# A decoder layer on one core: the residual stream kept with features on partitions, the norms' sums on TensorE, and the last gate in block products

## The chip, the cores and the metric

One Trainium2 chip, one of its cores. The metric is the device time of one launch in microseconds (us), lower is better: the median of three runs. All inputs lie in HBM (DRAM) when the launch begins, and the output must be there at its end.

## The reference, cut to what matters

One layer (DEPTH 1, batch 1) works on x of 1024 tokens by 1024 features, all in float32:

```python
def rms_norm(x, g):
    return x * lax.rsqrt(jnp.mean(x * x, axis=-1, keepdims=True) + EPS) * g
def swiglu(h, w_gate, w_up, w_down):
    return (jax.nn.silu(h @ w_gate) * (h @ w_up)) @ w_down

x = x + 0.5 * swiglu(rms_norm(x, ffn1_norm), ffn1_w_gate, ffn1_w_up, ffn1_w_down)   # hidden width 2816
h = rms_norm(x, mix_norm)
...                                     # h @ w_in, two attentions of 8 heads of 64, two sigmoid gates
x = x + merged @ w_out
x = x + 0.5 * swiglu(rms_norm(x, ffn2_norm), ffn2_w_gate, ffn2_w_up, ffn2_w_down)
x = x + sigmoid(rms_norm(x, ple_norm) @ w_ple_gate) * (p @ w_ple_proj)              # p: 1024 x 256
```

So there are four norms over the features, each ahead of a matrix product, and the residual x is read and written by every stage.

## The kernel before, in words

**Numbers.** A float32 matrix is split into a rounded part (`hi`, written by ScalarE as fp32r) and the rest (`lo`, a subtraction, mostly on VectorE): `split` at L104, whose two instructions stand in the profile at L105 and L106. A product takes three passes, hi times hi, hi times lo and lo times hi, so one 128x512 result over four blocks of 128 features is 12 matmuls.

**Seven products.** The large products are cut into two by two blocks and done with seven block products instead of eight, from sums of blocks. `make_up` (L474) does this for products whose input is a normed x: for each block n of 256 output columns, products m = 1 to 7, of 12 matmuls each (L556), in the order of `up_order`. Block 0 alone is done with all eight (`plain`, L506, 24 matmuls per result). The moving operands of the seven products are sums of the four blocks of h (two halves of 512 tokens by two halves of the features): `combo_a` makes the blocks of the second half of tokens, `combo_t` and `combo_l` the operand of product 5, `combo_u` and `combo_s` those of products 6 and 7, `combo_d` and `combo_e` that of product 4. Of these, the sums and the lo parts run on VectorE (L581 for lo parts, L617, L618, L626, L631, L632, L645, L646), the hi parts on ScalarE. `prep` splits a stationary weight tile (L105, L106), and `sums` (L521 to L523) forms sums of weight blocks. `make_down` (L363) does the same for the products that end in the residual: matmuls at L454, with the result added to the residual X from PSUM by VectorE at L462 (`evict`).

**The layout.** X is held as two halves of 512 tokens, each a tile of 128 tokens by 4 by 1024 features, tokens on partitions. A norm sums over one partition's row: ScalarE squares with a running sum (`norm_stat`, L215), GpSimd adds EPS and takes the power -0.5 on one column (L219, L220), VectorE multiplies by the gain (`norm_mul`, L223, 128x1024). The products need features on partitions, so `turn` (L228) transposes each normed tile on TensorE into PSUM, eight 128x128 transposes per 128 tokens, and the split into hi and lo reads PSUM (L105, L248 on ScalarE, L106, L253 on VectorE).

**The stages.** There are four entries, places where a norm feeds a `make_up` or, at the last, a plain product: FFN1 at the start (`first_entry`, L1426), the mix stage at about 650 us (`mix_start`, L1188), FFN2 at about 1520 us (`second_entry`, L1531), and the last stage at about 2160 us (`ple_start`, L1606). In the last three, the norm of the first half runs beside the last three products of the down product before it (`up_step`, L311: i counts the seven products, t the four results in one), and the second half's norm beside the first products after it (`up_first`, L330; `products`, L268). In `first_entry`, x comes in by pieces of 512 KB on SyncE's queue. The gain row is spread over the partitions by two fp32 matmuls (L190), and four bf16 matmuls (L204) follow. The last stage has no block products: `ple_steps` (L1586) does 16 results of 24 matmuls each at L1598, the last of them cut in pieces of 256, 128 and 128 columns, and finishes each with a sigmoid, a multiplication by a projection of p (from DRAM, L1582), an addition of X and an output DMA of 256 KB or less (L1601 to L1604).

**What sets the order.** The program order of each engine is the order of the code: every stage named here runs under a manual schedule. TensorE takes its matmuls strictly in that order, and so do VectorE, ScalarE and GpSimd; a wait of one instruction holds all behind it on its engine. The input and output DMAs go out from SyncE in order.

Of the kernel before, what the change touches and what calls it, by code (L numbers as in the profile page):

```python
# [18 lines left out]
P = 128  # L19
S = 1024  # L20
# [16 lines left out]
def tile_hybrid_decoder_layer(  # L37
# [118 lines left out]
    nc.vector.memset(mhalf[:], -0.5)  # L156

    xd = dp.tile([S, D], F32, name="x_mid")
    pd = dp.tile([S, D], F32, name="p_proj")
# [4 lines left out]

    def norm_begin(X, gain, first=None):
        if first is None:
            gB = slot("PT", [P, D])
            nc.sync.dma_start(gB[:], gain.partition_broadcast(P))
        else:
            gB = first["g"]  # L170
        return {"x": X, "g": gB, "hi": slot("H", [P, KD, 512], F32R), "lo": slot("H", [P, KD, 512], F32R), "h": {}, "r": {}}

    def combo_begin(X, gain, first=None, row=False):

        if first is None:
            gB = slot("PT", [P, D])
            if row:
                nc.scalar.dma_start(gB[0:1, :], gain.unsqueeze(0))
            else:
                nc.sync.dma_start(gB[:], gain.partition_broadcast(P))  # L180
            return {"x": X, "g": gB, "h": {}, "r": {}, "B": [slot("H", [P, 2, 4, 512], F32R) for _ in range(2)]}
        return {"x": X, "g": first["g"], "h": {}, "r": {}}

    def spread(gB):

        ones = slot("T", [1, P])
        nc.vector.memset(ones[:], 1.0)
        banks = [bank("sc") for _ in range(2)]
        for i, ps in enumerate(banks):
            pe(nc.tensor.matmul(ps[:], ones[:], gB[0:1, i * 512:i * 512 + 512], start=True, stop=True))  # L190
        for i, ps in enumerate(banks):
            nc.vector.tensor_copy(gB[:, i * 512:i * 512 + 512], ps[:])
# [3 lines left out]
    def busy(n):  # L196

        if not zero:
            zero.append(slot("T", [P, 512], BF16))
            nc.vector.memset(zero[0][:], 0.0)  # L200
            return
        ps = bank("av")
        for _ in range(n):
            pe(nc.tensor.matmul(ps[:], zero[0][:, 0:P], zero[0][:], start=True, stop=True))  # L204

    def norm_pre(N, t, tag="PT"):
        norm_stat(N, t, tag)
        norm_mul(N, t)

    def norm_stat(N, t, tag, first=False):  # L210
        xt = N["x"][:, t, :]
        h = N["h"][t] = slot(tag, [P, D])
        ss = stat([P, 1], "ss")
        rs = N["r"][t] = stat([P, 1], "rs", 8)
        nc.scalar.activation(h[:], xt, AF.Square, scale=D ** -0.5, accum_out=ss[:])  # L215
        if first:
            nc.scalar.activation(ss[:], ss[:], AF.Copy, bias=EPS)
        else:
            nc.gpsimd.tensor_scalar(ss[:], ss[:], EPS, None, ALU.add)  # L219
        nc.gpsimd.tensor_tensor(rs[:], ss[:], mhalf[:, 0:1], ALU.pow)  # L220

    def norm_mul(N, t):
        nc.vector.scalar_tensor_tensor(N["h"][t][:], N["x"][:, t, :], N["r"].pop(t)[:], N["g"][:], ALU.mult, ALU.mult)  # L223

    def turn(h, b, ps):
        for c in range(4):
            k = 4 * b + c
            pe(nc.tensor.transpose(ps[:, c * P:(c + 1) * P], h[:, k * P:(k + 1) * P], identf[:]))  # L228
        return ps[:].rearrange("p (c t) -> p c t", c=4)

    def norm_post(N, t, new_bank):
        h = N["h"][t]
        cs = slice(t * P, (t + 1) * P)
        for b in range(2):
            v = turn(h, b, new_bank())
            if "B" in N:
                split(N["B"][b][:, 0, :, cs], N["B"][b][:, 1, :, cs], v, nc.scalar, nc.vector)
            else:
                ks = slice(4 * b, 4 * b + 4)
                split(N["hi"][:, ks, cs], N["lo"][:, ks, cs], v, nc.scalar, nc.vector)  # L240

    def norm_high(N, t, new_bank):

        cs = slice(t * P, (t + 1) * P)
        N["v"] = N.get("v", {})
        N["v"][t] = [turn(N["h"][t], b, new_bank()) for b in range(2)]
        for b in range(2):
            nc.scalar.copy(N["B"][b][:, 0, :, cs], N["v"][t][b])  # L248

    def norm_low(N, t):  # L250
        cs = slice(t * P, (t + 1) * P)
        for b, v in enumerate(N["v"].pop(t)):
            nc.vector.tensor_sub(N["B"][b][:, 1, :, cs], v, f(N["B"][b][:, 0, :, cs]))  # L253

    def posts(N, at, new_bank):
        side = {}
        for t, i in enumerate(at):
            side.setdefault(i, []).append(lambda t=t: norm_post(N, t, new_bank))
        return side

    def halves(N):
        return [lambda a, k, n=n: n[("hi", "lo")[a]][:, k, :] for n in N]

    def finished(X, dst, half, t):
        row = half * 512 + t * P
        nc.sync.dma_start(dst[row:row + P, :], X[half][:, t, :])

    def products(F, rest=()):  # L268

        F.load(2)  # L270
        for i in range(2):
            F.plain(1, 0, (i,))
            for q in rest[i:i + 1]:
                F.a(q)
            F.prep(1, 1 + i)
        F.prep(1, 5)
        ps = F.product(1, 1)
        F.t(0)
        F.evict(1, 1, ps)
        F.t(1)  # L280
        F.l(0)
        ps = F.product(1, 2)
        F.t(2)
        F.prep(2, 1)
        F.l(1)
        F.t(3)
        F.l(2)
# [12 lines left out]
        F.s(3, 6)  # L300
        F.prep(1, 6)

    def up_begin(N, X, gain, F, i):

        if i == 3:
            N.append(combo_begin(X[0], gain))
            N.append(combo_begin(X[1], None, N[0]))
        elif i == 6:
            F.load(0)

    def up_step(N, X, dst, F, i, t):  # L311

        if i == 4:
            finished(X, dst, 0, t)
            norm_stat(N[0], t, ("WL", "WL", "WL", "WH")[t])
        elif i == 5:
            norm_mul(N[0], t)
        elif i == 6:
            finished(X, dst, 1, t)
            if t == 3:  # L320
                norm_post(N[0], 2, ps1)
            norm_stat(N[1], t, ("PT", "PT", "WH", "KL")[t])
            if t:
                if t < 3:
                    norm_mul(N[1], t - 1)
                norm_post(N[0], (None, 0, 1, 3)[t], ps1)
            if t == 2:
                F.prep(0, 1)

    def up_first(N, F):  # L330

        norm_mul(N[1], 2)
        F.load(1)
        F.a(0)
        norm_mul(N[1], 3)
# [1345 lines left out]
```

## Time and profile before

| what | number |
|---|---|
| median of three runs | 2263.56 us (2262.96 to 2263.61) |
| the profiled execution's own time | 2264.1 us |
| its span, first to last instruction | 2262.4 us |
| TensorE (PE) busy | 2235.7 us, 99% |
| VectorE (DVE) busy | 1486.8 us, 66% |
| ScalarE (ACT) busy | 989.3 us, 44% |
| GpSimd (POOL) busy | 801.2 us, 35% |
| mean granted TensorE clock | 0.999 of full speed |

The profile holds one execution, with the start and the duration of every instruction. A row of its timeline reads: start in us, duration or, where several instructions in a row are drawn together, their common length, engine, line, operation, tiles written and read, shape, count (x12), and in brackets the idle time of the engine ahead of it with what ended it. Two matmul records overlap, since a matmul's end is modelled; the pace of matmuls is read from the distance of starts. PEld is TensorE's weight load, which runs beside the matmuls. A busy share says how long an engine worked, not that it held up the end; for this the rows with brackets are read.

### The profile page before, as it was taken

To read this page: it belongs to the slowest core of one execution; us is meant where nothing else is said; L and a number is where in the kernel's file an instruction comes from. 1 tells how busy PE (TensorE), PEld (TensorE's weight loads), DVE (VectorE), ACT (ScalarE), POOL (GpSimd) and SP (SyncE) were. 2 spreads that over 40 slices of the span, in tenths; PEclk is the share of its full clock that TensorE was granted. 3 is DMA by queue.
4 is the path that set the end of the run, shared out by engine and by line. 5 is a ranking of instruction groups with operands and counts; after the bars stand their busy time and mean duration, and the time that the engine had idled before them with its cause. 6 is when DMAs were issued, how large, how long until landed. Compare 5 with 4: busy or idle time off the path is not lost. (4 is left out here: it accounts for less than half of the span.)

```text
span 2262.4 us, 30810 instructions
## 1 busy us (share of the span) xinstructions
PE 2235.7 (99%) x11402; PEld 1900.8 (84%) x11402; DVE 1486.8 (66%) x2303; ACT 989.3 (44%) x1788; POOL 801.2 (35%) x803
## 2 busy tenths in 40 slices
PE   8999999999999999999999999999999999999999
PEld 6888888888888899999898888888888888888888
DVE  8845555688888325666678875889655555778753
ACT  6333333333364445555566663345333333433431
POOL 2444444300011336565567664410544444200121
PEclk9999999999999999999999999999999999999999
DMA  4232323484233333233323366821423232756132
GB/s 140 102 117 85 125 84 125 145 311 172 84 131 113 127 109 110 85 113 85 85 66 91 106 196 232 283 106 55 140 89 121 84 126 84 268 191 217 59 102 85
DMA packets 188936, 291.23 MB, mean 129 GB/s; under 512 B 28393, under 2 KB 104553, under 8 KB 188786
## 3 DMA queue, kind: packets, MB, share of 16 engines
q1 hardware_dynamic: 188784, 289.26, 38.5%
q8 instruction: 90, 1.47, 0.3%
q14 instruction: 60, 0.49, 0.1%
q10 hardware_dynamic: 2, 0.00, 0.0%
HBM read 193.50 MB, written 78.94 MB: 120 GB/s over the span
## 5 line engine op out<-in xcount | busy, mean ns | idle before, releaser
L454 PE MATMUL ps<-H,H 128*128 128x512 f32 x2184 | 497.7, 389 | 1.2 <-DVE X L462 1.2
L454 PEld LDWEIGHTS ps<-H,H 128*128 128x128 f32 x2184 | 409.4, 188 | 86.6 <-issue 2.0
L556 PE MATMUL ps<-H,WL 128*128 128x512 f32 x1116 | 264.9, 389 | 0.8 <-ACT WL L105 0.8
L556 PEld LDWEIGHTS ps<-H,WL 128*128 128x128 f32 x1116 | 209.4, 188 | 44.6 <-ACT WL L105 1.2
L556 PE MATMUL ps<-H,Q 128*128 128x512 f32 x612 | 146.0, 389 | 0.0
L462 DVE SCALAR_TENSOR_TENSOR X<-ps,X 128x512 f32<-128x512 f32 x168 | 109.1, 687 | 50.9 <-PE ps L454 50.9
L556 PEld LDWEIGHTS ps<-H,Q 128*128 128x128 f32 x612 | 114.9, 188 | 23.8
L556 PE MATMUL ps<-X,WL 128*128 128x512 f32 x552 | 132.6, 389 | 0.0
L139 POOL TENSOR_TENSOR WL<-RAW,WH 128x512 fp32r<-128x512 f32 (+1 forms) x84 | 98.5, 1194 | 69.1 <-ACT WH L129 43.2
L556 PEld LDWEIGHTS ps<-X,WL 128*128 128x128 f32 x552 | 103.6, 188 | 21.5
L1121 DVE TENSOR_TENSOR PT<-ps,PT 128x512 fp32r<-128x512 f32 (+1 forms) x160 | 100.0, 627 | 30.9 <-ACT PT L1115 29.7
L799 PE MATMUL ps<-WH,H 128*128 128x256 f32 x768 | 116.1, 288 | 0.8 <-ACT RN L864 0.8
L807 PE MATMUL ps<-H,WH 128*128 128x512 f32 x384 | 115.1, 406 | 0.0
L219 POOL TENSOR_SCALAR ss<-ss 128x1 f32<-128x1 f32 x28 | 9.0, 323 | 296.1 <-ACT WL L215 231.9
L1139 PE MATMUL ps<-PT,X 128*128 128x256 f32 (+1 forms) x640 | 102.7, 286 | 6.9 <-DVE PT L1121 5.8
L556 PE MATMUL ps<-H,PT 128*128 128x512 f32 x456 | 108.9, 389 | 0.0
L1115 ACT CAST PT<-ps 128x512 fp32r<-128x512 f32 (+1 forms) x160 | 87.1, 548 | 42.2 <-PE ps L1113 40.7
L1139 PEld LDWEIGHTS ps<-PT,X 128*128 128x128 f32 x640 | 90.3, 190 | 17.6 <-DVE PT L1121 10.8
L799 PEld LDWEIGHTS ps<-WH,H 128*128 128x128 f32 x768 | 101.4, 190 | 2.7 <-ACT RN L864 1.2
L556 PEld LDWEIGHTS ps<-H,PT 128*128 128x128 f32 x456 | 85.5, 188 | 17.8
L355 POOL TENSOR_TENSOR PT<-GF,RN 128x512 f32<-128x512 f32 x20 | 33.6, 1682 | 184.9 <-DVE GF L710 184.9
L1067 POOL TENSOR_TENSOR T<-T,l 128x128 f32<-128x128 f32 (+3 forms) x64 | 73.2, 1148 | 72.1 <-DVE l L1066 70.0
(436 smaller groups left out, 4889.0 us busy)
## 6 DMA issues: line engine op xcount, KB each, us to landing
hidden<-PT SPq DMA_DIRECT2D x40, 512.0 KB, 3.0
WH<-in_ffn_w_gate_dram SPq DMA_DIRECT2D x38, 512.0 KB, 5.5
Q<-hidden SPq DMA_DIRECT2D x24, 512.0 KB, 5.5
hidden<-RN SPq DMA_DIRECT2D x22, 512.0 KB, 2.6
KH<-in_ffn_w_up_dram SPq DMA_DIRECT2D x20, 512.0 KB, 6.2
KL<-in_ffn_w_up_dram SPq DMA_DIRECT2D x20, 512.0 KB, 6.8
T<-in_ffn_w_down_dram SPq DMA_DIRECT2D x20, 512.0 KB, 7.5
X<-in_x_dram SPq DMA_DIRECT2D x16, 512.0 KB, 10.2
```

The costliest lines, as they stand in the source:

```text
L139: ins = eng_lo.tensor_sub(lo[part], raw[part], f(hi[part]))
L219: nc.gpsimd.tensor_scalar(ss[:], ss[:], EPS, None, ALU.add)
L355: eng.tensor_add(s12[:, 0, :], g1[:, 1, :], g2[:, 1, :])
L454: pe(nc.tensor.matmul(groups[g][t][:], act[:, a, k, t * P:(t + 1) * P], wt[:, b, k, :], start=(fresh and n == 0), stop=(i in (6, 1, 4) and ...
L462: nc.vector.scalar_tensor_tensor(xs, groups[g][t][:], scale, xs, ALU.mult, ALU.add)
L556: pe(nc.tensor.matmul(ps[:], hl[:, a, k, :], rhs(m, b, k), start=(first and i == 0), stop=(final and i == 11), skip_group_check=True))
L799: pe(nc.tensor.matmul(ps[:, :n], hT[t // 4](a, k)[:, (t % 4) * P:(t % 4 + 1) * P], w[k // 4][b][:, k % 4, :n], start=(i == 0), stop=(i == ...
L807: pe(nc.tensor.matmul(ps[:], w[a][:, k, :], hT[half](b, k), start=(i == 0), stop=(i == 23)))
L1067: nc.gpsimd.tensor_mul(T[:, :n], T[:, :n], l[:].broadcast_to([P, n]))
L1115: high = nc.scalar.copy(pt[:, 0, :width], ps[:, :width])
L1121: ins = nc.vector.tensor_sub(pt[:, 1, :width], ps[:, :width], f(pt[:, 0, :width]))
L1139: pe(nc.tensor.matmul(o, lh, r, start=(kpair == c and i == 0), stop=(kpair == 0 and i == 3)))
```

## The change

The residual is held with features on partitions from the first load to the output: X is now `[P, KD, 512]` for each half, KD = 8 blocks of 128 features by 512 tokens. The host transposes x, p and the output and reorders the gains; in DRAM the middle residuals, the projection of p and the output have the features outermost.

```diff
 def product / matmuls (make_down; the operands change places)
-pe(nc.tensor.matmul(groups[g][t][:], act[:, a, k, t * P:(t + 1) * P], wt[:, b, k, :], ...
+pe(nc.tensor.matmul(groups[g][t][:], wt[:, b, k, t * P:(t + 1) * P], act[:, a, k, :], ...
 def evict
-xs = X[half][:, t, d * 512:d * 512 + 512]
+xs = X[half][:, d * 4 + t, :]
```

The norm's sum now runs over partitions. ScalarE squares each 128x512 block; GpSimd (VectorE for the last) adds the eight squares; four fp32 matmuls by a column of ones give the sums of 512 tokens as a 128x4 tile; VectorE adds EPS, GpSimd takes the power; and four TensorE transposes of the broadcast column give a 128x512 tile in PSUM whose rows are all alike. VectorE multiplies X by gain and this row, block by block. No normed data are transposed.

```diff
-    def turn(h, b, ps):
-        for c in range(4):
-            k = 4 * b + c
-            pe(nc.tensor.transpose(ps[:, c * P:(c + 1) * P], h[:, k * P:(k + 1) * P], identf[:]))
...
+    def norm_sq(N, k, eng=nc.gpsimd):
+        d = norm_at(N, k)
+        nc.scalar.activation(d, N["x"][:, k, :], AF.Square, scale=D ** -0.5)
...
+            eng.tensor_add(N["acc"], N["acc"], d)
...
+    def norm_sum(N, ps):
+        acc = N.pop("acc")
+        for t in range(4):
+            pe(nc.tensor.matmul(ps[:, t:t + 1], acc[:, t * P:(t + 1) * P], ones1[:], start=True, stop=True))
+        rs = N["r"] = stat([P, 4], "rs")
+        nc.vector.tensor_scalar(rs[:], ps[:, 0:4], EPS, None, ALU.add)
+        nc.gpsimd.tensor_tensor(rs[:], rs[:], mhalf[:, 0:4], ALU.pow)
...
+    def norm_row(N, ps):
+        rs = N.pop("r")
+        for t in range(4):
+            pe(nc.tensor.transpose(ps[:, t * P:(t + 1) * P], rs[:, t:t + 1].broadcast_to([P, P]), identf[:]))
+        N["row"] = ps
...
+    def norm_mul(N, k):
+        nc.vector.scalar_tensor_tensor(norm_at(N, k), N["x"][:, k, :], N["g"][:, k:k + 1], N["row"][:], ALU.mult, ALU.mult)
```

The combos of `make_up` now go by feature block k instead of token block q, on 128x512 blocks in SBUF. `combo_b` (the lo parts) is split off `combo_a`, one of its two subtractions going to GpSimd; `combo_u` is split in u (in `products` on GpSimd) and v; and v, the hi and the lo part of product 6's operand follow each other for each k.

```diff
 def products
-        F.plain(0, 1)
-        F.u(0)
-        F.u(1)
-        F.s(0, 6)
-        F.s(1, 6)
-        F.prep(2, 2)
-        F.plain(1, 1)
-        F.u(2)
-        F.u(3)
-        F.s(2, 6)
-        F.s(3, 6)
+        for k in range(4):
+            F.t(k)
+            if k:
+                F.l(k - 1)
+                F.u(k - 1, nc.gpsimd)
+        F.l(3)
+        F.u(3, nc.gpsimd)
+        F.plain(0, 1)
+        for k in range(4):
+            F.v(k)
+            F.s(k, 6)
+        F.prep(2, 2)
+        F.plain(1, 1)
         F.prep(1, 6)
```

`first_entry` loads x in pieces of 256 KB, one per feature block, squares each, and issues one fp32 matmul of 128x512 with a zero stationary operand on each piece that has come (`busy`, L232 of the kernel after); both bf16 and gain matmuls of before are gone. The last stage becomes a `make_up` of four column blocks: block 0 with `plain`, 96 matmuls, and three blocks of 84. Its results are finished by `finish`, a multiplication and an addition with tiles of the projection and of the residual (which now makes a round trip through DRAM) that a DMA brings in: for blocks 0 to 2 on GpSimd over 128x1024, for the last block on VectorE over 128x512.

```diff
+        def finish(n, i, e, hs=slice(0, 2), eng=nc.gpsimd, more=True):
+            pt, xt = T[n, i]
+            eng.tensor_mul(e[:, hs], e[:, hs], pt[:, hs])
+            eng.tensor_add(e[:, hs], e[:, hs], xt[:, hs])
+            nc.sync.dma_start(out[0, (2 * n + i) * P:(2 * n + i + 1) * P, :].rearrange("p (h n) -> p h n", h=2)[:, hs], e[:, hs])
...
+            seqn = up_order(4)
+            for s, (n, m) in enumerate(seqn):
+                evict(n, m, F.product(n, m))
```

TensorE at the start of the program, before. PT, WL and Y hold normed tokens, H the operands, L506 is `plain`:

```order
L190 MATMUL ps_110<-PT_101,T_107 128x512
L204 MATMUL ps_158<-T_105 128x512
L228 MATMUL ps_163<-identf,PT_130 128x128 x4
...
L228 MATMUL ps_211<-identf,PT_151 128x128 x4
L506 MATMUL ps_237<-H_103,WL_189 128x512 x12
L506 MATMUL ps_237<-H_104,WL_228 128x512 x12
L228 MATMUL ps_289<-identf,Y_220 128x128 x4
...
L506 MATMUL ps_338<-H_103,WL_258 128x512 x12
```

The same place after the change. X is the residual, PT and Q the sums of squares of the two halves, rs the 128x4 column, L482 is now `plain`:

```order
L232 MATMUL ps_117<-X_101,T_115 128x512 x8
L199 MATMUL ps_161<-ones_86,PT_134 128x1 x4
L208 MATMUL ps_169<-identf,rs_166 128x128 x4
L482 MATMUL ps_209<-H_175,WL_184 128x512 x12
L482 MATMUL ps_209<-H_176,WL_199 128x512 x12
L482 MATMUL ps_259<-H_175,WL_206 128x512 x12
L199 MATMUL ps_272<-ones_86,Q_225 128x1 x4
L482 MATMUL ps_259<-H_176,WH_222 128x512 x12
L208 MATMUL ps_296<-identf,rs_277 128x128 x4
L532 MATMUL ps_335<-H_175,PT_280 128x512 x12
```

The first product moved behind the sum and the row of the whole first half, where before it stood behind transposes of single token blocks; and the second half's sum and row stand between whole products.

VectorE in `products` of FFN1, before, from the second `combo_u` on. Q, KH and KL hold the second half's blocks, RN and GF the sums, H_493 is product 6's operand:

```order
L631 TENSOR_TENSOR Q_308<-Q_308 128x512
L632 TENSOR_TENSOR Q_308<-Q_308,RN_425 128x512
L581 TENSOR_TENSOR H_493<-Q_288,H_493 128x4x128
L581 TENSOR_TENSOR H_493<-Q_308,H_493 128x4x128
L106 TENSOR_TENSOR WL_498<-WH_335,WL_498 128x512
L631 TENSOR_TENSOR KH_351<-KH_351 128x512
```

The same place after (L601 is v, L554 a lo part, H_427 product 6's operand):

```order
L601 TENSOR_TENSOR Q_225<-Q_225,RN_378 128x512
L554 TENSOR_TENSOR H_427<-Q_225,H_427 128x512
L601 TENSOR_TENSOR Q_227<-Q_227,RN_378 128x512
L554 TENSOR_TENSOR H_427<-Q_227,H_427 128x512
L601 TENSOR_TENSOR KH_230<-KH_230,GF_387 128x512
L554 TENSOR_TENSOR H_427<-KH_230,H_427 128x512
```

The four u of before left VectorE, and each lo part now follows the v that it reads, with a hi part on ScalarE between them.

GpSimd from the first power on, after the change (L202 the power, L221 lo parts of the first half, L191 the sum of squares of the second, L554 lo parts of product 3's operand, L598 u):

```order
L202 TENSOR_TENSOR rs_166<-rs_166,mhalf 128x4
L221 TENSOR_TENSOR H_176<-PT_154,H_176 128x512
L191 TENSOR_TENSOR Q_225<-Q_225,Q_227 128x512
...
L202 TENSOR_TENSOR rs_277<-rs_277,mhalf 128x4
L554 TENSOR_TENSOR T_303<-Q_225,T_301 128x512
...
L554 TENSOR_TENSOR T_304<-KL_233,T_302 128x512
L598 TENSOR_TENSOR Q_225<-Q_225 128x512
...
L598 TENSOR_TENSOR KL_233<-KL_233 128x512
```

Before, GpSimd did only one-column work in this place (L219, L220), and its next 128x512 operation was a weight sum at L526. Now 15 operations of 128x512 stand there: 2 of L221, 5 of L191, 4 of L554 and 4 of L598.

More of the change, by code (lines that the diff above doesn't have):

```diff
@@ L184, in spread, with norm_begin @@
[L184 to L192, printed above, removed]
+    def norm_begin(X, i, tags):
+        return {"x": X, "g": gains[:, i, :], "tags": tags, "s": {}}
@@ L200, in busy @@
             nc.vector.memset(zero[0][:], 0.0)
+            zero.append(bank("av"))
             return
[L202 to L220, printed above, removed]
@@ L261, in halves @@
[L261 to L275, printed above, removed]
-        F.prep(1, 5)
[L277 to L283, printed above, removed]
+        pe(nc.tensor.matmul(zero[1][:], zero[0][:], src, start=True, stop=True))
@@ L330, in up_first @@
+            for k in ((0, 1), (2, 3, 4), (5, 6), (7,))[t]:
+                norm_low(N[0], k, nc.gpsimd if k in (4, 5) else nc.vector)
     def up_first(N, F):
[L332 removed]
         F.load(1)
+        F.prep(0, 2)
+        F.plain(0, 0, (0,))
+        norm_sum(N[1], bank("sc"))
+        F.prep(0, 5)
+        F.prep(0, 4, nc.gpsimd)
+        F.plain(0, 0, (1,))
+        norm_row(N[1], bank("av"))
         F.a(0)
[L335 to L337 removed]
+        F.plain(1, 0, (0,))
@@ L1457, in first_entry @@
+        norm_sum(N[0], bank("pt"))
+        norm_row(N[0], bank("pf"))
+        for k in range(4):
+            norm_mul(N[0], k)
+            norm_high(N[0], k)
+        F.prep(0, 1)
+        for k in range(4):
+            norm_low(N[0], k)
+        for k in range(4, 8):
+            norm_mul(N[0], k)
+            norm_high(N[0], k)
         F.prep(0, 2)
-        norm_stat(N[1], 1, "Y")
+        for k in range(4, 8):
+            norm_low(N[0], k, nc.gpsimd if k in (5, 7) else nc.vector)
+        F.prep(0, 5)
```

500 lines of the change are left out of this document (237 added, 263 removed).

## The prediction, made before the changed kernel was run

> **What bounds the kernel now.** I read the page's busy line first, then the list of what each engine waited for, then TensorE's timeline.
>
> ```profile
> PE 2235.7 (99%) x11402; PEld 1900.8 (84%) x11402; DVE 1486.8 (66%) x2303; ACT 989.3 (44%) x1788; POOL 801.2 (35%) x803
> ```
>
> ```profile
> PE ps L1139 <- DVE PT L1121: 5.8, 13, 1.3
> PE ps L1113 <- DVE PT L1121: 4.3, 6, 1.2
> PE ps L190 <- DMA PT<-in_ffn_norm_dram: 3.6, 1, 3.6
> PE ps L228 <- DVE H L106: 2.0, 3, 1.0
> PE ps L506 <- DVE H L253: 1.3, 1, 1.3
> ```
>
> Out of 2262.4 us TensorE idles 27, and the longest waits (total, times, longest) lie in the attention, which the change leaves alone. So the kernel is bound by TensorE, and a saving counts only if operands still come in time. VectorE's 66% is an average. At the FFN1 entry, where the change moves most, it is full (columns: PE, PEld, DVE, ACT, POOL):
>
> ```profile
> 20.00:40.00 20.00, 20.00 (x106) 16.89 (x105) 19.14 (x32) 14.23 (x32) 4.60 (x3) 1.00 0.26 80
> 40.00:60.00 20.00, 19.23 (x86) 15.58 (x85) 18.61 (x30) 10.69 (x20) 0.00 (x0) 1.00 0.00 1
> ```
>
> There VectorE works 19 of 20 us just to keep up, and GpSimd nothing. That is the place to watch.
>
> **TensorE's own work.**
>
> ```profile
> 22.17 1.91 PE L228 MATMUL ps<-identf,Y 128*128 128x128 f32 x16
> 23.83 2.99 PE L506 MATMUL ps<-H,WL 128*128 128x512 f32 x12
> 53.93 5.74 PE L556 MATMUL ps<-H,WL 128*128 128x512 f32 x24 [0.77 <-ACT WL L105]
> 59.50 2.88 PE L556 MATMUL ps<-X,WL 128*128 128x512 f32 x12
> 2165.25 1.20 PE L1598 MATMUL ps<-WH,H 128*128 128x512 f32 x4
> 2250.63 0.40 PE L1598 MATMUL ps<-WH,H 128*128 128x256 f32 x2
> 2258.59 0.39 PE L1598 MATMUL ps<-PT,H 128*128 128x128 f32 x2
> ```
>
> Sixteen transposes take 23.83 − 22.17 = 1.66 us, 0.104 each; 24 matmuls of 128x512 about 5.44, 0.2267 each (12 in 2.72). In the entries of mix, FFN2 and the last stage 192 transposes go: −20.0. The last stage's 360 matmuls of 128x512 and the three narrower pieces (2250.63 to 2258.8: 8.2) are 81.6 + 8.2 = 89.8; 96 + 3 x 84 = 348 are 78.9: −10.9. Added are six half-norms of 4 fp32 matmuls by one column and 4 transposes. A 128x1 matmul is in no row; I price its two records like transposes (12 x 0.104 = 1.25; from 0.4, only the transposes counted, to 3.1 if a record costs as much as a 512 one): +1.3 each, +7.8. Sum of work: −23.1. Were a row's duration taken for its cost, these transposes would be worth more: the Trainium skill, "TensorE: Matmul & The Clock Gate", Part 4, puts one PE transpose in a kernel at about 275 ns. This trace agrees with that as a record's length (16 end 1.91 us after the first began) but not as pace; by 275 ns the 192 would be 52.8 us and my total 33 lower, as an estimate. I go by the pace.
>
> **The price on VectorE and GpSimd.** The seven products' operands are made by VectorE, by dependent 128x512 operations:
>
> ```profile
> 35.09 0.69 DVE L617 TENSOR_TENSOR RN<-Q,H 128x512 f32<-128x512 f32 x1
> 35.81 0.69 DVE L618 TENSOR_TENSOR RN<-RN,H 128x512 f32<-128x512 f32 x1
> 36.42 0.69 DVE L617 TENSOR_TENSOR RN<-Q,H 128x512 f32<-128x512 f32 x1
> 109.14 0.62 ACT L105 CAST WL<-WH 128x512 fp32r<-128x512 f32 x1
> ```
>
> An operation starts 0.72 after the one that it reads, else 0.61. A cast on ScalarE is 0.62. From `norm_row` of the second half to the product (1,6), VectorE now has in program order: 8 `norm_mul` (4.9), 4 lo parts (2.4), 5 splits of weights (3.1; 6 in the last three entries, 3.7), 3 sums (2.2), one eviction (0.6), 8 subtractions of `combo_t` (5.3), 4 lo parts of product 5 (2.4). Then comes the new loop of v, hi on ScalarE, lo, each waiting for the one before: 0.69 + 0.04 + 0.62 + 0.04 + 0.61 = 2.0, four times, 8.0. v of the next block stands behind lo of this one, so ScalarE's cast can't be covered. Together 28.9.
>
> New on GpSimd in this stretch are 8 operations of 128x512, 4 lo parts (L554) and 4 u (L598). They are not free to VectorE:
>
> ```profile
> 107.81 0.69 DVE L106 TENSOR_TENSOR WL<-KH,WL 128x512 fp32r<-128x512 f32 x1
> 109.72 1.29 POOL L356 TENSOR_TENSOR PT<-PT,GF 128x512 f32<-128x512 f32 x1
> 109.80 1.76 DVE L106 TENSOR_TENSOR WL<-WH,WL 128x512 fp32r<-128x512 f32 x1 [1.31 <-ACT WL L105]
> 110.97 1.75 POOL L357 TENSOR_TENSOR PT<-GF 128x512 f32<-128x512 f32 x1
> 111.49 1.78 DVE L106 TENSOR_TENSOR WL<-KL,WL 128x512 fp32r<-128x512 f32 x1
> 114.72 0.69 DVE L690 TENSOR_TENSOR RN<-RN,ps 128x512 f32<-128x512 f32 x1 [1.46 <-ACT RN L689]
> ```
>
> The same L106 takes 0.69 alone and 1.76 beside a GpSimd operation; one that reads PSUM (L690) is not held. So each GpSimd operation costs VectorE 1.07, 0 to 8.6 for eight; two of the eight lie beside `norm_mul`, which reads PSUM, so 6.5. With 1.2 for two last casts: 28.9 + 6.5 + 1.2 = 36.6, and 37.2 in the last three entries. There TensorE has 120 matmuls in the same stretch (72 of `plain`, products (1,1), (1,2), (1,5), (2,1)), 27.2. It will idle 10.0.
>
> **Mix, FFN2, last stage.** Two smaller waits come in each. `norm_sum` puts an instruction into VectorE's queue (L201) behind the splits of the next down operand, 128x1024 each:
>
> ```profile
> 445.10 4.17 DVE L106 TENSOR_TENSOR H<-RAW,H 128x1024 fp32r<-128x1024 f32 x2
> 446.04 2.15 POOL L356 TENSOR_TENSOR KH<-KH,GF 128x512 f32<-128x512 f32 x1
> 449.19 2.30 DVE L106 TENSOR_TENSOR H<-KH,H 128x1024 fp32r<-128x1024 f32 x1
> 660.82 1.28 DVE L581 TENSOR_TENSOR H<-Q,H 128x512 fp32r<-128x512 f32 x2
> 5.89 0.56 POOL L220 TENSOR_TENSOR rs<-ss,mhalf 128x1 f32<-128x1 f32 x1 [4.03 <-ACT ss L217]
> ```
>
> Four splits at about 1.2 undisturbed (two operations of 512 are 1.28), an eviction 0.7, L201 and the power 0.8: 6.1 beside 12 matmuls, 2.7, and some start-up: 2.6 idle, 0 to 4, with `norm_row`, a down result of 12 matmuls and its eviction queued behind on TensorE. The second half's sum costs 0.7 likewise. So 2.6 + 0.7 + 10.0 = 13.3 idle for each entry. What idled there before, 2.0 (L228 row), goes. Mix: −6.7 (64 transposes) + 2.6 + 13.3 − 1.0 = +8.2. FFN2: the same, +8.2. Last stage: −6.7 − 10.9 + 2.6 + 13.3 = −1.7. Besides, blocks 0 to 2 are finished there by 12 GpSimd operations of 128x1024. The rows at 445 to 449 show VectorE's 1024 at 2.1 to 2.3 instead of 1.2 beside such work, so 12 x 1.0 = 12 at the most, 0 at the least; VectorE has some 30 operations (20 us) in 41 us of matmuls, so a third of the holds hits idle time: +8. And the end gets longer:
>
> ```profile
> 2255.03 5.27 SPq L1604 DMA_DIRECT2D out_dram<-KH  x3
> ```
>
> Before, 3.6 us lay between the last matmul and the end, with pieces of 64 KB and operations of 0.29. Now the last results are 128x512 (sigmoid 0.62, two operations 0.7, 256 KB), while block 2's two 1024 operations hold them (1.0 each) and their 512 KB goes ahead on SyncE: +5, from 1 to 8. Last stage and end: +11.3.
>
> At nothing I cost the swap of operands at L454 (as many matmuls of the same shape), the squares in pieces on ScalarE, and the residual's way through DRAM in the last stage, under this cover:
>
> ```profile
> 2165.00:2250.00 85.00, 84.91 (x392) 70.48 (x391) 31.61 (x42) 19.71 (x31) 13.74 (x12) 1.00 0.35 118
> ```
>
> ```profile
> Q<-hidden SPq DMA_DIRECT2D x24, 512.0 KB, 5.5
> ```
>
> ScalarE works 20 of 85 us there and the DMA engines 35%; a tile asked for one result ahead (5.4 us of matmuls) about covers the 5.5 us of a 512 KB load, and if not, it is GpSimd's `finish` that is late, not TensorE.
>
> **The first entry.**
>
> ```profile
> 3.58 3.75 PE L190 MATMUL ps<-PT,T 1*128 1x512 f32 x4 [3.58 <-DMA PT<-in_ffn_norm_dram]
> 9.30 1.06 ACT L215 ACTIVATE PT<-X 128x1024 f32<-128x1024 f32 x1
> 9.49 1.66 PE L228 MATMUL ps<-identf,PT 128*128 128x128 f32 x8 [0.35 <-DVE PT L223]
> 10.99 1.04 PE L228 MATMUL ps<-identf,WL 128*128 128x128 f32 x8
> 15.01 2.11 PE L506 MATMUL ps<-H,WL 128*128 128x512 f32 x8 [0.24 <-ACT H L248]
> ```
>
> The first half of x is in by 9.3. Eight fp32 matmuls are 16 records; four take 3.7 us at the start, 0.9 each, and the pace doubles at about 10.7 (the transposes at 9.49 against those at 10.99). From 4.4, 7 records by 10.7, 9 more at 0.45: 14.7 (12.5 if the clock is up sooner). Sum 0.9, L201 and power 0.8, row 0.5: 16.9. Four `norm_mul` with casts and a weight cast, 3.6: first product at 20.5, before 15.01. Its second part needs 13 VectorE operations (7.9) and casts from 16.9 on, and one more wait: 27.3. ScalarE's squares of the second half stand behind weight casts that wait for VectorE's last lo parts: first pair at 31.6. Then five GpSimd additions (1.37), two on VectorE (1.5): 39.9. Before that, TensorE has run out at about 33. Sum 1.0, 12 matmuls 2.7, row 0.5: 44.1. Plus the chain of 36.6: product (1,6) at 80.7. Before it began at 53.93 behind the same products: **+26.8**.
>
> **Sum.** 26.8 + 8.2 + 8.2 + 11.3 = +54.5 on the profiled 2264.1: 2318.6. The median is 0.5 below that execution: **2318**, 2.4% slower.
>
> **Rivals.**
> 1. *TensorE cools in the new gaps.* Its pace doubles only 7.1 us after the first matmul (3.58 to 10.7), and in this trace no gap after the start was longer than 1.3, so nothing shows what a gap of 3 to 7 us does. If it halves the pace for the next stretch: the sum, 12 matmuls and the row in FFN1, +4, and about 3 in three other entries, +9: 2331. The page named above, "Why this matters for your kernels", has this rule, with gaps over some 3 us; only the start here bears on it.
> 2. *No mutual hold.* The held rows may come of those tiles, not of GpSimd. Then 4 x 6.5 and the 8 go: 2318 − 34 = 2284.
> 3. *Faster: VectorE works ahead of TensorE.* If second-half work is done so early that the chain from the row falls under TensorE's 27.2 us, which decides it, each entry loses only its sum: 2264.1 − 23.1 − 2.0 + 5.5 (first product) + 5 (end) = 2249. Against it stand the full windows above: VectorE has no slack at this place, and the loop of 8.0 is serial.
>
> **How the numbers follow.** Forecast 0.57 (2296 to 2332), cooling 0.25 (2322 to 2342), no hold 0.10 (2275 to 2296), hidden 0.08 (2244 to 2266). The forecast's own width is that of its unknowns (hold −6.5 to +2.1 in four entries, finish −8 to +4, end −4 to +3), few of which will lie at one end together. The range reaches from 2296 to 2342 and leaves out the last two. About 0.2%, 4.5 us, is what a measurement of this kernel can tell from no change: faster 0.06, same 0.02 (the upper end of hidden), slower 0.92.
>
> **What would show it.** First L482 at about 20 us; TensorE idle near 33 to 40 behind L191; L532 of (1,6) at 75 to 85 after a wait on L551 or L106; VectorE's L590 and L554 rows at 1.7 beside GpSimd's L598; three entries with 10 to 15 us idle; an end of 7 to 9 us after the last matmul. I am wrong if those VectorE rows stay at 0.69, or if TensorE's idle total stays under 50 us.

## The result, and the profile after

| | before | after | difference |
|---|---|---|---|
| median of runs | 2263.26 us | 2334.79 us (2332.39 to 2336.52) | ratio 1.0315 (1.0297 to 1.0333) |
| profiled execution | 2264.1 us | 2336.5 us | +72.4 |
| span | 2262.4 us | 2334.8 us | +72.4 |
| mean granted TensorE clock | 0.999 | 0.987 | |

The kernel became 3.2% slower; 2.4% (+54.5 us) was forecast. 2334.8 lies in the range given (2296 to 2342), but above the forecast's own stretch (up to 2332), in that of the first rival. The busy line of the page and the head of TensorE's list of waits (total, times, longest), after the change:

```profile
PE 2244.5 (96%) x11166; PEld 1888.5 (81%) x11166; DVE 1555.3 (67%) x2354; ACT 1003.1 (43%) x1782; POOL 911.6 (39%) x832
```

```profile
PE ps L532 <- ACT WL L105: 15.2, 4, 5.1
PE ps L208 <- POOL rs L202: 8.6, 4, 2.4
PE ps L199 <- DVE Q L191: 6.4, 4, 4.8
```

TensorE's idle time grew from 27 to 90 us, and nearly every new wait is one on a norm's sum (L199, L208) or on an operand of the block products; 3.0 us are waits for a result to leave its bank. Its busy time did not fall either, although it has 236 matmul records fewer: the eight fp32 matmuls at the start (L232) count 9.7 us, and busy time counts a matmul longer at a lower clock (24 of them 7.34 us at 83.72 below, 5.60 at 1562.15 before). The wait of four times put down to ScalarE's cast (L105) is that of product (1,6) in the four entries; the cast is only the last of a chain.

TensorE's timeline of the first entry, after:

```profile
4.22 9.71 PE L232 MATMUL ps<-X,T 128*128 128x512 f32 x16 [4.22 <-DMA X<-in_x_dram]
13.77 0.95 PE L199 MATMUL ps<-ones,PT 128*128 128x1 f32 x8
16.07 0.94 PE L208 MATMUL ps<-identf,rs 128*128 128x128 f32 x4 [1.36 <-POOL rs L202]
21.00 5.49 PE L482 MATMUL ps<-H,WL 128*128 128x512 f32 x12 [3.98 <-ACT WL L105]
...
40.51 1.87 PE L199 MATMUL ps<-ones,Q 128*128 128x1 f32 x8 [4.77 <-DVE Q L191]
42.24 5.20 PE L482 MATMUL ps<-H,WH 128*128 128x512 f32 x12
47.28 0.60 PE L208 MATMUL ps<-identf,rs 128*128 128x128 f32 x4
...
83.72 7.34 PE L532 MATMUL ps<-H,WL 128*128 128x512 f32 x24 [3.28 <-ACT WL L105]
```

The first product starts at 21.0 (15.0 before), the second half's sum at 40.5 after a wait of 4.8, and (1,6) at 83.7. Where the time was lost is read from the start of product (1,6) in each entry, the place at which the two kernels go on alike. The rows of the later entries, after:

```profile
735.82 4.62 PE L532 MATMUL ps<-T,WL 128*128 128x512 f32 x12 [3.39 <-ACT WL L105]
1567.50 2.88 PE L482 MATMUL ps<-H,WL 128*128 128x512 f32 x12
1613.10 7.34 PE L532 MATMUL ps<-H,WL 128*128 128x512 f32 x24 [3.40 <-ACT WL L105]
2218.20 2.88 PE L482 MATMUL ps<-H,WL 128*128 128x512 f32 x12
2269.66 4.34 PE L532 MATMUL ps<-X,WL 128*128 128x512 f32 x12 [5.12 <-ACT WL L105]
2324.60 2.89 PE L532 MATMUL ps<-H,WL 128*128 128x512 f32 x12
```

and of the same products before:

```profile
694.68 3.03 PE L556 MATMUL ps<-T,WL 128*128 128x512 f32 x12
1562.15 5.60 PE L556 MATMUL ps<-H,WL 128*128 128x512 f32 x24
```

| up to | before | after | lost in this part | forecast |
|---|---|---|---|---|
| (1,6) of FFN1 | 53.93 | 83.72 | 29.8 | 26.8 |
| (1,6) of the mix stage | 694.68 | 735.82 | 41.1 − 29.8 = 11.4 | 8.2 |
| (1,6) of FFN2 | 1562.15 | 1613.10 | 51.0 − 41.1 = 9.8 | 8.2 |
| the end | 2262.4 | 2334.8 | 72.4 − 51.0 = 21.4 | 11.3 |

VectorE and GpSimd ahead of (1,6) of FFN1, after:

```profile
64.12 1.78 DVE L590 TENSOR_TENSOR RN<-Q,H 128x512 f32<-128x512 f32 x1
65.93 0.69 DVE L591 TENSOR_TENSOR RN<-RN,H 128x512 f32<-128x512 f32 x1
66.54 1.78 DVE L554 TENSOR_TENSOR H<-RN,H 128x512 fp32r<-128x512 f32 x1
...
74.88 0.68 DVE L601 TENSOR_TENSOR Q<-Q,RN 128x512 f32<-128x512 f32 x1
76.24 0.69 DVE L554 TENSOR_TENSOR H<-Q,H 128x512 fp32r<-128x512 f32 x1 [0.69 <-ACT H L551]
76.85 0.68 DVE L601 TENSOR_TENSOR Q<-Q,RN 128x512 f32<-128x512 f32 x1
78.22 0.69 DVE L554 TENSOR_TENSOR H<-Q,H 128x512 fp32r<-128x512 f32 x1 [0.68 <-ACT H L551]
```

```profile
63.62 1.73 POOL L598 TENSOR_TENSOR Q<-Q 128x512 f32<-128x512 f32 x1 [4.42 <-PE ps L482]
65.98 1.80 POOL L598 TENSOR_TENSOR Q<-Q 128x512 f32<-128x512 f32 x1 [0.63 <-DVE RN L590]
```

Both forecast mechanisms stand here to be read: an L590 or L554 takes 1.78 beside each u of GpSimd (L598) and 0.69 without, and the loop of v and lo takes 76.85 − 74.88 = 1.97 us a block, with VectorE idle 0.69 in each for ScalarE's cast.

Last, the clock. The same stretches by window (the columns are start and end, length, busy time of PE, PEld, DVE, ACT and POOL, then PEclk), after:

```profile
36.00:48.00 12.00, 7.49 (x26) 6.32 (x27) 2.23 (x5) 0.79 (x2) 4.19 (x4) 0.72 0.01 2
82.00:92.00 10.00, 8.28 (x29) 6.69 (x30) 9.49 (x16) 6.37 (x13) 0.00 (x0) 0.83 0.01 2
735.00:741.00 6.00, 5.18 (x16) 4.09 (x17) 5.70 (x10) 4.90 (x11) 0.00 (x0) 0.72 0.56 179
668.00:676.00 8.00, 5.57 (x21) 4.31 (x20) 4.82 (x7) 1.59 (x3) 2.28 (x2) 0.79 0.17 66
1545.00:1551.00 6.00, 3.57 (x18) 2.70 (x19) 5.08 (x7) 3.26 (x5) 1.13 (x2) 1.00 0.01 4
```

Behind the longer gaps the granted clock falls, to 0.72 to 0.83 in the mean of such a window, and the 24 matmuls at 83.72 take 7.18 us (to the next start, 90.90) for 5.44. So the first rival came true beside the forecast. The last two rows hold one gap of 2.43 us each, the wait of L208 in the mix stage and in FFN2: behind the first the clock fell, behind the second it did not.

### The profile page after: what moved, and what is told of

Same layout as the page of the kernel before. It is cut to its first block, busy times and chain, and to the rows that moved or that the text cites. A ratio compares the mean times of both kernels' runs of the same rounds, so it can differ in the third digit from the quotient of the medians.

```text
span 2334.8 us, 30467 instructions
## 1 busy us (share of the span) xinstructions
PE 2244.5 (96%) x11166; PEld 1888.5 (81%) x11166; DVE 1555.3 (67%) x2354; ACT 1003.1 (43%) x1782; POOL 911.6 (39%) x832
## 4 chain that ended last, share of the span: by engine, by line
PE 78%; DVE 10%; issue 5%; ACT 3%; POOL 2%; DMA 1%; SPq 0%; POOLq 0%; DVEq 0%; ACTq 0%
PE ps L532 37%; PE ps L434 17%; PE ps L765 7%; PE ps L773 4%; PE ps L1368 3%; PE ps L1106 3%; PE ps L1080 2%; PE ps L1022 1%; PE ps L1021 1%; DVE H L106 1%; PE ps L927 1%; DVE PT L1088 1%; DVE RN L984 1%; DVE H L554 1%; DVE GF L984 1%
## 5 line engine op out<-in xcount | busy, mean ns | idle before, releaser
L532 PE MATMUL ps<-H,WL 128*128 128x512 f32 x1164 | 280.3, 393 | 7.6 <-ACT WL L105 6.7
L532 PEld LDWEIGHTS ps<-H,WL 128*128 128x128 f32 x1164 | 220.4, 190 | 55.5 <-ACT WL L105 7.5
L532 PE MATMUL ps<-H,Q 128*128 128x512 f32 x648 | 154.8, 389 | 3.1 <-DVE Q L106 3.1
L532 PE MATMUL ps<-X,WL 128*128 128x512 f32 x600 | 145.9, 392 | 6.0 <-ACT WL L105 5.1
L532 PEld LDWEIGHTS ps<-H,Q 128*128 128x128 f32 x648 | 121.5, 188 | 28.8 <-DVE Q L106 3.6
L532 PE MATMUL ps<-H,PT 128*128 128x512 f32 x516 | 132.0, 405 | 8.5 <-ACT H L551 5.0
L532 PEld LDWEIGHTS ps<-X,WL 128*128 128x128 f32 x600 | 113.3, 189 | 31.0 <-ACT WL L105 5.6
L532 PEld LDWEIGHTS ps<-H,PT 128*128 128x128 f32 x516 | 100.0, 196 | 35.1 <-ACT H L551 6.7
L191 POOL TENSOR_TENSOR WL<-WL 128x512 f32<-128x512 f32 x3 | 3.9, 1300 | 313.3 <-ACT WL L189 313.3
```

The costliest lines, as they stand in the source:

```text
L532: pe(nc.tensor.matmul(ps[:], hl[:, a, k, :], rhs(m, b, k), start=(first and i == 0), stop=(final and i == 11), skip_group_check=True))
```

## The experiments

My theory: VectorE's chain from the second half's row to (1,6) sets each entry, long by a serial loop and by GpSimd's hold, and gaps add a slow clock. The rivals: the casts on ScalarE, the layout itself, or VectorE's mere amount of work. Each kernel is the changed one with the edit named; e4, e5, e11 and e12 change several things at once, and a part of their edits is printed. All medians stand against 2334.8 of the changed kernel and 2263.3 to 2264.3 of the kernel before.

### The serial loop

```diff
         for k in range(4):
             F.v(k)
+        for k in range(4):
             F.s(k, 6)
```

> The four v come first, then the four hi and lo parts of product 6's operand. By my theory (the loop of v, cast, lo is serial, and VectorE's chain sets product (1,6)) the chain falls from 8.0 to about 5.4 us in each entry, 4 x 2.6 = 10 us, and up to 7 more where the gap ahead of (1,6) becomes too short to slow TensorE: 10 to 17 us faster than the changed kernel, about 2318 to 2325. By the rival that ScalarE's casts of the weights set it (they release TensorE in the trace), the order on VectorE does nothing: within 3 us of 2335.

Measured: 2319.09 us, 15.7 faster. VectorE in this run:

```profile
73.52 1.28 DVE L602 TENSOR_TENSOR Q<-Q,RN 128x512 f32<-128x512 f32 x2
...
75.93 1.28 DVE L555 TENSOR_TENSOR H<-Q,H 128x512 fp32r<-128x512 f32 x2
```

Eight operations follow each other without a gap, 73.52 to 78.34, 4.8 us for 7.9, and (1,6) no longer waits in FFN1, the mix and FFN2. ScalarE's cast as the limit falls: the same cast comes earlier when VectorE does. So does VectorE's mere amount of work, which is the same in both.

### GpSimd's hold

```diff
-                F.u(k - 1, nc.gpsimd)
...
-        F.u(3, nc.gpsimd)
```

> Leaves out the four u of each entry on GpSimd, so product 7's operand lacks one difference of blocks. GpSimd is not on any path there, so only a hold of VectorE by GpSimd can make this faster. By the theory of the mutual hold 4 x 1.07 = 4.3 us in each of four entries, 17 us, and up to 7 more from the clock: 2311 to 2318. Without a hold: within 3 us of 2335.

Measured: 2321.66, 13.1 faster, 3.3 an entry in the mean, by taking four operations an entry off an engine for which nobody waits there. The hold is real. It fell short of 17: in the profiled executions the last entry gave only 1.2 (from (1,6) of FFN2 to the end 720.5 us for 721.7), and in the other three a gap of 4.3 us ahead of (1,6) was still there and the clock fell behind it (in FFN1 24 matmuls took 7.86 us for 7.18). A version that keeps the result is the same edit with u on VectorE behind the split of (1,6); v goes to the tile of the sums and ScalarE copies it back:

```diff
+        F.prep(1, 6)
+        for k in range(4):
+            F.u(k)
+            F.c(k)          # ScalarE: copy of v
```

> u moves from GpSimd to VectorE, behind the weight split of (1,6); v is kept in the tile of the sums until then and copied back by ScalarE. By the hold the chain loses 4 x 1.07 = 4.3 us in each entry (e2 gave 13 in all), and the four u cost 2.4 where VectorE comes behind (1,6): 5 to 13 us faster, 2322 to 2330, if they are covered there. If VectorE is as full behind (1,6) as ahead of it, they come back as waits of products (1,7) and (2,6), and the gain is 17 - 10 = 7 at most, or none.

Measured: 2325.97, 8.8 faster. (1,6) of FFN1 comes at 78.05 where e2 had it at 78.32, and (1,6) of FFN2 at 1599.5 for 1600.1: up to there the four u on VectorE are covered, and the gain of e2 is kept whole. What was given back lies behind that: in the last stage TensorE waits 5.0 us for ScalarE's copy of a result out of its bank (L1577 of e8; 0.8 in e2), which stands behind the copies of v, and these behind u:

```profile
2266.08 5.16 PE L533 MATMUL ps<-X,WL 128*128 128x512 f32 x12 [4.96 <-ACT GF L1577]
```

In the two profiled executions this comes to 1.8 us in the end (from (1,6) of FFN2 722.3 for 720.5). The medians lie 4.3 apart, with e8's runs between 2323.5 and 2329.4; the rest of the 4.3 is not explained.

### The clock

> Matmuls into an unused PSUM bank fill three gaps of TensorE: after the first row (8 of fp32), ahead of the second sum in FFN1 (20), and ahead of product (1,6) in all four entries (14). Nothing that the kernel computes waits for them longer than the gap lasted. By the theory that the gaps slow TensorE's matmuls for a while, the slow matmuls behind them come back to 0.227 us: about 7.5 us in FFN1 and 1.7 in the others, 12 us faster than the changed kernel, 2323. If the slow matmuls have another cause: 2335 or a few us more.

```diff
+            if (n, m) == (2, 1):
+                filler(N[1]["row"], 14)     # 128x512, into a bank that nobody reads any more
```

Measured: 2330.31, 4.5 faster instead of 12. This is the same stretch behind (1,6) as above, with the fillers:

```profile
82.00:92.00 10.00, 10.00 (x46) 8.27 (x45) 9.86 (x17) 5.46 (x11) 0.00 (x0) 1.00 0.00 0
```

The clock there is 1.00 for 0.83, and the 24 matmuls of (1,6) and (2,2) take 5.51 us for 7.18 (81.34 to 86.85). So where a gap is filled the slow matmuls go, and the cause is shown. The sum was wrong for two reasons: the 8 fp32 fillers lasted to 22.2 and held the first product, and gaps that were left kept 0.86 and 0.87 in the windows 36 to 48 and 69 to 82: 1.9 us ahead of the second sum, where the 20 fillers did not last (the 12 matmuls behind it took 4.0 us for 5.0), and 1.3 us inside the product ahead of the other fillers.

### The last stage

e4 replaces the stage by 16 results of 24 matmuls in the new layout, with X still in SBUF (in e4 the last column block multiplies by sums of weight blocks instead of the blocks).

```diff
+            for n in (0, 1):
+                result(n, 0, 1)
+                result(n, 1, 1)
...
+            nc.scalar.activation(e, ps[:], AF.Sigmoid)
+            nc.vector.tensor_mul(e, e, T[n, f_][:, half, :])
+            nc.vector.tensor_add(e, e, Xs[half][:, q, :])
```

> The last stage alone goes back to 16 results of 24 matmuls with X from SBUF, in the new layout: 384 matmuls (87 us) for 348 (79 us), no combos but those of the second half's blocks, no GpSimd finish, no DRAM round trip of the residual. By my theory (stage lost to VectorE's chain, GpSimd's hold, a late load) the stage takes about 95 us from its first matmul to the end for 116.6: 21 us faster, 2314. By the rival that the layout's norm alone makes the loss, it gains 5 us or less.

Measured: 2322.08, 12.7 faster; the stage took 101.6 us (2217.4 to 2319.0) for 116.6, with one wait of 4.6 us behind weight splits that I had put behind the combos. e5 puts them ahead:

> As e4, with the last column block's own weights (e4 took sums of blocks there) and block 1's weight splits ahead of the second half's combos, so that TensorE's wait of 4.6 us behind them goes. Last stage from its first matmul to the end in 95 to 98 us, where the changed kernel takes 116.6 and e4 took 101.6: 2314 to 2317. If the layout's second half itself is late for the plain products too, the wait moves to the results of the second half and 2322 stays.

Measured: 2314.78, 20.0 faster, as expected, so the layout's norm alone is not what the stage lost. 36 matmuls more (8.2 us) gain 20 us: what comes with the seven products, their operands and finishes on VectorE and GpSimd, the waits and the slow clock behind them, cost 28. Two runs look for it:

```diff
-                r = T[n, i] = [slot(t, [P, 2, 512]) for t in (("KH", "KH") if (n, i) == (2, 0) else ("T", "Y"))]
+                r = T[n, i] = [slot(t, [P, 2, 512]) for t in (("KH", "KH") if (n, i) == (3, 0) else ("T", "Y"))]
-                if (n, i) == (2, 1):
+                if (n, i) == (1, 0):
                     fetch()
```

> The last stage's tile for its result (3,0) is loaded into other buffers, one finish earlier, so that it doesn't wait for GpSimd's addition and an output DMA. VectorE waits 7.1 us for that load in the changed kernel, with the weight splits of the last three products queued behind. If this is a part of what the last stage lost, TensorE's 3.2 and 0.6 us there and the slow matmuls behind them go: 4 to 6 us faster, 2329 to 2331. If GpSimd's finish is the limit there anyway: 2335.

Measured: 2334.03, no change (from (1,6) of FFN2 to the end 721.5 us for 721.7). In the changed kernel VectorE waits 7.1 us for this load, and it looked like a part of the loss:

```profile
2315.75 0.69 DVE L1553 TENSOR_TENSOR GF<-GF,T 128x512 f32<-128x512 f32 x1 [7.08 <-DMA T<-p_proj]
```

With the load early, VectorE did the same work at once, and beside GpSimd's finish it took (e9):

```profile
2309.84 1.51 DVE L1553 TENSOR_TENSOR GF<-GF,KH 128x512 f32<-128x512 f32 x1 [0.70 <-ACT GF L1582]
2311.38 2.77 DVE L1554 TENSOR_TENSOR GF<-GF,KH 128x512 f32<-128x512 f32 x1
2314.07 2.87 DVE L106 TENSOR_TENSOR Q<-RAW,Q 128x512 fp32r<-128x512 f32 x1
```

The wait was gone, and the hold took its place: TensorE's wait for the split of the next weights (Q) fell only from 3.2 to 1.3 us, and the end did not move. The load was no cause. Then the finish itself:

```diff
-        def finish(n, i, e, hs=slice(0, 2), eng=nc.gpsimd, more=True):
+        def finish(n, i, e, hs=slice(0, 2), eng=nc.vector, more=True):
```

> The last stage's twelve multiplications and additions of 128x1024 go from GpSimd to VectorE. They cost VectorE 12 x 1.2 = 14 us, and by the hold they cost it up to 12 x 2.5 where they run on GpSimd beside its work. By the hold the stage gets faster although VectorE has more to do: 3 to 8 us, 2327 to 2332, with the end shorter too. Without it VectorE only gets more work: slower, up to 2345.

Measured: 2325.83, 9.0 faster, though VectorE has twelve operations more, 14.7 us by their rows; its busy time even fell, from 1555.3 to 1553.5 us. Why shows in the rows ahead of (1,6), first the changed kernel's VectorE and GpSimd, then e10's VectorE:

```profile
2254.16 4.52 DVE L554 TENSOR_TENSOR T<-X,T 128x512 fp32r<-128x512 f32 x2
2258.60 2.85 DVE L601 TENSOR_TENSOR Q<-Q,X 128x512 f32<-128x512 f32 x1
```

```profile
2255.47 2.66 POOL L1553 TENSOR_TENSOR GF<-GF,T 128x1024 f32<-128x1024 f32 x1
2258.21 2.69 POOL L1554 TENSOR_TENSOR GF<-GF,Y 128x1024 f32<-128x1024 f32 x1
```

```profile
2253.36 2.36 DVE L554 TENSOR_TENSOR T<-X,T 128x512 fp32r<-128x512 f32 x2
2255.64 1.21 DVE L1553 TENSOR_TENSOR GF<-GF,T 128x1024 f32<-128x1024 f32 x1
2256.89 1.23 DVE L1554 TENSOR_TENSOR GF<-GF,Y 128x1024 f32<-128x1024 f32 x1
2258.03 0.69 DVE L601 TENSOR_TENSOR Q<-Q,X 128x512 f32<-128x512 f32 x1
```

A VectorE operation of 512 that meets one of 1024 on GpSimd lasts as long as that one, 2.85 beside 2.69: it loses 2.2, more than if VectorE did the 1024 operation itself (1.2). Ahead of (1,6) the two nearly even out (50.1 us from the first plain product for 51.5). Most of the gain lies behind it (57.9 us from (1,6) to the end for 65.1): there TensorE's waits fall from 6.1 us to 1.9, and VectorE's two operations held at 2269 to 2275 (2.56 and 2.89) take 0.7 each.

### The sums

```diff
-            elif t == 1:
+            elif t == 2:
...
-            for k in ((), (0, 1), (2, 3, 4), (5, 6, 7))[t]:
+            for k in ((), (), (0, 1, 2, 3), (4, 5, 6, 7))[t]:
```

> The first half's row is issued one down result later in the mix, FFN2 and last entries. If the sum's wait (2.4 us behind the splits on VectorE) is only a matter of place, 3 x 2.4 = 7.3 us go: 2327. If VectorE is too late anyway (its norm_mul now start 2.7 us later), the wait comes back ahead of the first plain product: 2335.

Measured: 2327.10, 7.7 faster, the price of three waits of L208, which were only a matter of place.

```diff
+        for k in range(KD):
+            norm_sq(N[1], k)
...
-        for k in range(KD):
-            norm_sq(N[1], k, nc.vector if k > 5 else nc.gpsimd)
```

> In the first entry the second half's squares and additions come ahead of the first half's multiplications, the additions all on GpSimd. If the second sum is late because ScalarE's squares stand behind the weight casts, the wait of 4.8 us and the slow matmuls behind it go, and as the chain from the row to (1,6) keeps its length, the row's 10 us of lead reach (1,6): 8 to 10 us faster, 2325 to 2327. By the rival that VectorE's total work up to (1,6) sets it, whatever the row's place: 2 us or less.

Measured: 2334.45, no change within the spread of the runs (in the profile (1,6) of FFN1 came 3.5 us sooner, the end 1.9). The wait ahead of the second sum went, but another came ahead of the first product, and this is ScalarE in e7:

```profile
14.87 1.31 ACT L189 ACTIVATE Q<-X 128x512 f32<-128x512 f32 x2 [3.03 <-DMA X<-in_x_dram]
...
19.66 0.63 ACT L189 ACTIVATE KL<-X 128x512 f32<-128x512 f32 x1
20.19 1.12 ACT L217 CAST H<-PT 128x512 fp32r<-128x512 f32 x2
```

The second half of x is there only at 14.9, so the squares held the first half's casts, and the first product came at 22.9. The second row came at 43.7 for 47.3, and from there to (1,6) it took 36.5 us, in the changed kernel 36.4. So the chain keeps its length wherever it begins, but the edit did not begin it the 10 us sooner that I counted on. By the time alone (0.3 us) the rival, VectorE's total work up to (1,6), would fit; against it stands that VectorE idles 5.0 us ahead of the second sum in e7.

### Together

e11 joins e1, e5, e6 and e8, puts the second half's squares on ScalarE between the casts of the first half, with their sums on GpSimd and VectorE, puts the weight sums behind the combo of block 3 (F.b), and fills the gaps of the first entry:

```diff
-            busy(X[0][:, k, :])
...
+        busy(16)            # 128x512 bf16
...
+        busy(8)
...
+            nc.scalar.activation(norm_at(N[1], k), X[1][:, k, :], AF.Square, scale=D ** -0.5)
...
-        F.sums(1, nc.vector)
         F.b(3)
+        F.sums(1, nc.vector)
```

> All that helped: v ahead of the parts, u on VectorE behind (1,6), the row later, the last stage plain, the lo part b(3) ahead of the weight sums; and the first entry with bf16 matmuls that wait for no data in place of the fp32 ones, squares of the second half between the first half's casts, their additions shared by GpSimd and VectorE. From 2334.8 by my terms: 20 (stage), 7.5 (row), 21 (split and u in three entries, with the clock), 8 to 12 (first entry): 2275, 2268 to 2290, still not under 2264, since the first product stays behind the sum of all features. If the terms don't add (VectorE as full behind (1,6)): 2290 to 2300.

Measured: 2283.62, 51.2 faster than the changed kernel and 0.9% slower than the kernel before (1.0073 to 1.0103). TensorE in e11:

```profile
72.71 5.60 PE L535 MATMUL ps<-H,WL 128*128 128x512 f32 x24
713.24 3.06 PE L535 MATMUL ps<-T,WL 128*128 128x512 f32 x12 [0.24 <-ACT WL L105]
1583.15 5.74 PE L535 MATMUL ps<-H,WL 128*128 128x512 f32 x24 [0.24 <-ACT WL L105]
2188.83 2.88 PE L1578 MATMUL ps<-H,WL 128*128 128x512 f32 x12
```

Against before, (1,6) is late by 18.8, 18.6 and 21.0 us in FFN1, mix and FFN2, the end by 21.1. Of the loss that is left, 18.8 of 21.1 lie in the first entry. Its first product comes at 21.0 for 15.0, behind a sum over all features: that is 6.0. The other 12.8 come between the first product and (1,6), where TensorE still waits 9.7 us for operands and runs some matmuls at the lower clock.

e12 is e11 with the seven products kept in the last stage, VectorE's finish of e10 and the early load of e9:

```diff
-        def finish(n, i, e, hs=slice(0, 2), eng=nc.gpsimd, more=True):
+        def finish(n, i, e, hs=slice(0, 2), eng=nc.vector, more=True):
...
-                if (n, i) == (2, 1):
+                if (n, i) == (1, 0):
```

> As e11, but the last stage by seven products, with its finishes on VectorE and the early load. If only the hold and the serial loop ate the gain of the 36 matmuls saved, the stage now takes some 87 us for e11's 94.7: 2276. If VectorE's chain ahead of (1,6) and its 12 finishes of 1.2 us are as long as the stage's matmuls allow, the saving is given back as waits behind (1,6) and at the end: 95 to 99 us, 2284 to 2288. I hold the second likelier, since e10's end and its wait at block 3 came from VectorE.

Measured: 2292.94, 9.3 slower than e11 and later than either expectation; the stage took 103.8 us (2186.6 to 2290.4) for 94.7. TensorE waits 9.5 us in it between its second result and product (1,7), and its last matmul is 7 us before the end. With four column blocks the seven products did not pay in any of the orders tried.

## Why the prediction was right, and where it was off

- **What bounds it, and the sign.** Right: TensorE lost in waits more than the 23 us of work that it saved. The third rival (VectorE works ahead, faster) and the second (no hold) fall by e1, e2 and e10. "GpSimd nothing" at the FFN1 entry before holds for the second of the two windows shown only; the first has 4.60 us. Nothing else was worked out from it.
- **TensorE's own work.** The transposes' pace held. A sum cost 0.8 to 0.9 us and a row 0.4 at full clock, 1.2 to 1.3 where 1.3 was put.
- **The chain to (1,6).** 36.6 us were forecast from the row on in FFN1; 47.28 to 83.72 are 36.4. In FFN2 it took 38.4 (from 1574.68) for 37.2. Its parts stood too: 1.97 a block in the loop (2.0), about 1.09 lost for each u (1.07).
- **The first entry.** First product 21.0 (20.5), second sum 40.5 (39.9), (1,6) 83.7 (80.7). The 3 us between are the slow clock at 42.24, where 12 matmuls took 5.04 us.
- **Mix and FFN2.** Lost 11.4 and 9.8 for 8.2: the clock behind the gap ahead of the previous entry's (1,6) adds 1.7 in each, and in the mix it fell behind the wait of L208 too, where the stretch from that row to the first plain product took 1.4 longer than in FFN2 (671.97 to 690.25, 1550.64 to 1567.50). The waits on the two sums, 2.6 and 0.7 forecast, are 2.4 and 0.5.
- **The last stage is the term that was mis-sized**, 21.4 for 11.3; 4.9 of the 10.1 between them are the slow clock (below). The step "12 x 1.0 = 12 at the most" priced the hold by rows in which VectorE's operation was of 1024 and GpSimd's of 512; here it is the other way round. VectorE's 512 beside GpSimd's 1024 loses 2.2, and the first block's finish stood in the chain to (1,6): from the first plain product to (1,6) it took 51.5 us there and 45.6 in FFN2. The end grew by 3.9 (7.5 from the last matmul to the end, for 3.6), where 5 was put. What I costed at nothing, the way through DRAM, did make a load late, but in e9, with the load early, the end stayed where it was.
- **The clock** was a rival with 0.25 and 13 us, and should have been a term. Adding the slow groups on the path (42.24: 2.3, the sum ahead of it 0.9, behind L208 in the mix 1.4, (1,6): 1.7, 1.7, 1.7 and 1.5, the product at 2320: 1.7) gives 12.9, and 54.5 + 12.9 = 67.4 of 72.4. What is left, 5.0, lies in the last stage. So the time lies in the range because the range took in this rival; the sum alone gave 2318.

## What to carry to other kernels

An operation moved to an idle engine is not free if that engine shares something with the full one: price it by a row in which both run, and by the longer of the two. Where the saving is on the bounding engine, work out the chain that must feed it, with each round trip between engines inside it, before counting the saving; a loop of two engines per block costs the sum of both, two loops one after the other the longer one. And a sum over the whole input puts the first product behind the whole input: 6.0 us here, which no reordering in these runs brought back.

## What the runs showed of the hardware

- A VectorE operation with two SBUF inputs that meets a GpSimd one lasts about as long as that one: 1.78 beside 1.73 (128x512), 2.85 beside 2.69 (128x1024).
- The length of a gap alone does not say whether the granted clock falls. In the changed kernel it fell behind gaps of 2.52 us (0.79 in the window 725 to 733) and behind the 2.43 of L208 in the mix (0.79 in 668 to 676), not behind the 2.43 in FFN2 (1.00 in 1545 to 1551). In e3 a gap of 1.3 us was enough (0.87 in 69 to 82), while the kernel before, after its start, has gaps of up to 1.3 and none of them brought a fall. In e11 two gaps of 0.54 and 1.43 us, half a us apart, were enough:

```profile
64.00:73.00 9.00, 7.27 (x24) 5.63 (x25) 8.88 (x16) 5.32 (x10) 0.00 (x0) 0.81 0.00 0
```

- The low stretches are not of any length. In the changed kernel's trace the clock is either full or 0.50, for 3.41 us or two or three times that while TensorE has work, and the low stretches begin whole multiples of 3.41 us apart (16.29, 29.94, 40.18, 74.31, ..., 671.65, ..., 2320.28). So where a gap lies against these steps may decide; that was not tried.

The Trainium skill, "TensorE: Matmul & The Clock Gate", Why this matters for your kernels, warns of gaps over some 3 us; these runs agree in kind, and show falls behind shorter ones, of 1.3 to 2.5 us. How the share of busy time decides it was not tried.
